# Tokens loaded first, squares summed on TensorE, modulation blocks moved between the first projection steps

## The chip, the cores and the metric

One core of a Trainium2 chip runs the whole program in one launch. The metric is the device time of that launch in microseconds (us). The kernel before takes 2099.12 us (median of 3 runs, 2098.18 to 2099.53). The profiled execution took 2101.66 us, and its span, from the first to the last instruction in the trace, is 2099.9 us.

The engines are named as in the profile: PE is TensorE's matrix multiplication and PEld its weight load, DVE is VectorE, ACT is ScalarE, POOL is GpSimd. SP only issues transfers, and POOL issues the stores.

## The reference

Two layers of a diffusion trunk over 128 context tokens and 1024 latent tokens of width 1024. Everything the change touches lies in the opening of layer 0:

```python
def rms_norm(x, g):
    y = xf * lax.rsqrt(jnp.mean(xf * xf, axis=-1, keepdims=True) + EPS)
    return (y * g.astype(jnp.float32)).astype(x.dtype)
def ada_mod(cvec, w, b):
    m = jax.nn.silu(cvec) @ w + b
    shift, scale, gate = jnp.split(m, 3, axis=-1)
...
hp = rms_norm(xp, norm_w[l]) * (1.0 + sc_p) + sh_p
hs = rms_norm(xs, norm_w[l]) * (1.0 + sc_s) + sh_s
...
z_a, xbc, dt_raw, u_b, g_b = jnp.split(h @ w_in, SPLIT_E, axis=-1)
```

and in the filter of the Hyena channels, which needs no token at all:

```python
hdn = jnp.sin(freq * (feats @ w1 + b1))
hdn = jnp.sin(freq * (hdn @ w2 + b2))
filt = (hdn @ w3).astype(f32)
```

## The kernel before

Tokens lie along the free axis: a tile is 128 channels by T = 1158 columns (the context, two zero columns, the latents, four zero columns), and there are eight such tiles `x[0]` to `x[7]`, called `hl` in the trace because they sit in the buffers that later hold the low halves. Each float32 operand of a large product is split into a high and a low part, so a product is three matmuls (L158 to L160 in `proj`, L185 to L187 in `proj_step`).

The opening (L1444 to L1506) does these things, in this order of issue:

- `silu_wide` prepares the conditioning vectors (`cw`).
- `filter_mlp` is a generator with the two small layers of the filter's network. `KM = (-1, 2)` runs the first layer before everything else and the second one in the middle of the loop over the tokens. A layer is six matmuls (L401, L412), then `sin_layer` on DVE (L377 to L383) and the sine on ACT (L384). The second layer ends with its result split into `hdh` and `hdl` (L418, L419), from which all the filter's later work starts.
- Eight blocks of the modulation's weights, 1 MB each in two halves, are loaded by `load`. Block order is `(0, 4, 1, 5, 2, 6, 3, 7)`: a shift block and the scale block of the same two channel tiles. `ada` multiplies a block with `cw` (L288, 16 matmul records) and copies the row out (L294); `cols` turns rows into columns with a selection matrix (L304) and adds the bias on DVE (L307, and L311 for a scale).
- Blocks 0 to 3 are loaded alternately with the tokens: two halves of a block, then two token tiles, and so on.
- For each token tile ACT squares it (L1485) and DVE adds the square to `xacc` (L1487), seven additions one after the other.
- `rstd_rep` sums `xacc` over the partitions with nine matmuls that have one column each (L324, 18 records), turns the sums into 1/sqrt on POOL (`pow`, L330), and spreads the result over all partitions with three diagonal products (L336 on DVE, L339 on PE, copies L343 to L347 on ACT) into `rep`. Its argument `fill` slips `cols` and the fifth block between.
- For k = 0 to 7, `make_h` forms the normalized and modulated tile k: a product on DVE (L356), the high part on ACT (L361), the low part on DVE (L362), two zero stretches on POOL (L365, L366). `proj_step` then multiplies it with slices of the first two weight chunks, 18 matmuls per step. `cols` runs in each step, and `ada` in the first three.

Then comes the stage `xbc`: the first two chunks are evacuated and convolved (L582 to L594, L695, L696), and ten more chunks of 72 matmuls follow. Beside it a list of generators (`self.bg`) is advanced, one step for each third of a chunk (`tick`, rate `RX` = 1.0): `filter_groups`, eight groups of the filter (L496 to L571), ending each with a store to `Hd` on POOL's queue. When `xbc` is through, `drain` empties the list, the buffers of the filter are given back, and the stage `z` begins, whose own background work loads the remaining modulation weights (`wa`) into memory that the filter held.

PSUM has two pools: three banks `pj`, and five banks `bg` that the second chunk of the first projection shares with everything else. Each engine runs its own instructions strictly in the order in which they stand. That order is set by the tile framework's scheduler from the order of the code and its own estimates.

Of the kernel before, what the change touches and what calls it, by code (L numbers as in the profile page):

```python
# [9 lines left out]
AF = mybir.ActivationFunctionType  # L10
# [5 lines left out]
D = 1024  # L16
# [20 lines left out]
def tk(c):  # L37
    return 0 if c == 0 else OFF + 128 * (c - 1)
# [6 lines left out]
class Net:  # L45
    XE = "vector"
    MID, RA = 2, 2.5
    KM, RX = (-1, 2), 1.0
    NT, EX, RO, RH, RS, RZ = 1, 3, 1.6, 1.7, 1.4, 2.0
# [263 lines left out]

    def rstd_rep(self, acc, pool, ncnt, tag="tt", fill=()):

# [4 lines left out]
        nc = self.nc  # L320
        p = self.ps()
        one = self.ones[0:acc.shape[0], 0:1]
        for c in range(NCH):
            nc.tensor.matmul(p[:, c:c + 1], acc[:, tk(c):tk(c) + 128], one, start=True, stop=True)  # L324
        for f in fill[:-3]:
# [8 lines left out]
        for g in range(3):  # L334
# [10 lines left out]
            else:  # L345
                o = tk(3 * g)
                nc.scalar.copy(rep[:, o:o + 384], q[:, :384])  # L347
        return rep

    def make_h(self, l, k, x, rep, slot):  # L350
# [20 lines left out]
    def sin_layer(self, arg, src, bcol, fcol, pool):  # L371
# [11 lines left out]
        nc.vector.tensor_scalar(out=arg, in0=arg, scalar1=3.1415925, scalar2=-3.1415925, op0=ALU.min, op1=ALU.max)  # L383
        nc.scalar.activation(arg, arg, AF.Sin)  # L384

    def filter_mlp(self, keep, pool):
# [31 lines left out]
        nc.scalar.copy(hi, b)  # L418
        nc.vector.tensor_tensor(out=lo, in0=b, in1=hi.bitcast(F32), op=ALU.subtract)  # L419
        self.hdn = hi, lo  # L420

    def stage_a(self, s, d, rd, qd, A, pool, tag):
# [1000 lines left out]
    def run(self, upto="end"):  # L1423
# [19 lines left out]
        self.nraw = 0  # L1443
        mlp = self.filter_mlp(p_hf, p_fg)  # L1444
        self.bg.append(self.filter_groups(p_fg))
        with self.pool("x0") as px:
            x = [self.t(self.p_h, [128, T], f"hl{k}") for k in range(8)]
            self.silu_wide(px)
            acc = self.t(px, [128, T], "xacc")
            blocks = (0, 4, 1, 5, 2, 6, 3, 7)  # L1450
            raws = []

            def load(n):
                if n < 4:
                    r = [self.t(self.p_h, [128, 1024], f"hh{(2 * n + h) % 6}") for h in range(2)]
                elif n == 6:
                    r = [self.t(p_fg, [128, 1024], "u8", bufs=self.nu8) for h in range(2)]
                else:
                    t = self.t(p_fg, [128, 2048], "A") if n == 7 else self.t(p_fg, [128, 2304], "F", bufs=2)
# [3 lines left out]
                raws.append(r)  # L1463

            rows = []

            def ada(n):
                rows.append(self.ada_block(blocks[n], raws[n], px))

            def cols():  # L1470
                while rows:
                    self.ada_cols(*rows.pop(0))

            if -1 in self.KM:
                next(mlp)
            for n in range(4):
                load(n)
                for k in (2 * n, 2 * n + 1):
                    self.dma(x[k], self.i["xT"][:, k])
            for n in range(4):  # L1480
                cols()
                ada(n)
                for k in (2 * n, 2 * n + 1):
                    sq = self.t(self.p_h, [128, T], f"hh{6 + k % 2}") if k else acc
                    nc.scalar.activation(sq, x[k], AF.Square)  # L1485
                    if k:
                        getattr(nc, self.XE).tensor_tensor(out=acc, in0=acc, in1=sq, op=ALU.add)  # L1487
                if n in self.KM:
                    next(mlp, None)
            self.w_load(0)  # L1490
            load(4)
            load(5)
            self.w_load(1)
            load(6)
            load(7)
            self.load_tf(p_hf)
            nop = lambda: None
            rep = self.rstd_rep(acc, px, D, "xacc", [cols, lambda: ada(4), nop, nop, nop])
            self.ps0 = [[self.pj() for b in range(3)], [self.ps() for b in range(3)]]
            first = [(None, self.w_next(), p) for p in self.ps0]  # L1500
            for k in range(8):
                self.make_h(0, k, x[k], rep, (px, [128, T], "sq") if k % 2 else (self.p_h, [128, T], "hh7"))
                cols()
# [341 lines left out]
```

## Time and profile before

| | |
|---|---|
| median of 3 runs | 2099.12 us |
| profiled execution | 2101.66 us, span 2099.9 us |
| PE busy from 0 to 50 us | 27.2 of 50 us with gaps of up to 8.6 us |
| PE busy from 100 to 400 us | 297.4 of 300 us |
| DVE busy from 100 to 180 us | 74.6 of 80 us |
| matrix clock over the span | 0.989 of full |

How to read the profile: it is one execution recorded by the hardware. A row of the timeline gives the start in us, the duration in us, the engine, the line of the kernel, the operation, the tile written and the tiles read, how many instructions were merged into the row, and in brackets the idle time ahead of it and what ended it. A table by stretches gives the busy us of each engine with the number of instructions, then the granted clock of PE (PEclk, 1.00 is full) and what the transfers did. On PE one matmul of float32 shows as two records; a busy PE may still be slow, because its clock may be halved.

### The profile page before, as it was taken

To read this page: it belongs to the slowest core of one execution; us is meant where nothing else is said; L and a number is where in the kernel's file an instruction comes from. 1 tells how busy PE (TensorE), PEld (TensorE's weight loads), DVE (VectorE), ACT (ScalarE), POOL (GpSimd) and SP (SyncE) were. 2 spreads that over 40 slices of the span, in tenths; PEclk is the share of its full clock that TensorE was granted. 3 is DMA by queue.
4 is the path that set the end of the run, shared out by engine and by line. 5 is a ranking of instruction groups with operands and counts; after the bars stand their busy time and mean duration, and the time that the engine had idled before them with its cause. 6 is when DMAs were issued, how large, how long until landed. Compare 5 with 4: busy or idle time off the path is not lost.

```text
span 2099.9 us, 33885 instructions
## 1 busy us (share of the span) xinstructions
PE 2041.4 (97%) x13088; PEld 1839.9 (88%) x13088; DVE 1316.7 (63%) x2774; ACT 908.3 (43%) x2031; POOL 120.4 (6%) x241
## 2 busy tenths in 40 slices
PE   5999999999999999999999999999999999999998
PEld 2899998889999999888887899898888888888977
DVE  5797745135778788898899774644444344454464
ACT  3576552252333332554466512434445454453231
POOL 1110001110000000000000000200000000000000
PEclk8999999999999999999999999999999999999999
DMA  8133339654121213343353451423333223333462
GB/s 331 52 124 102 117 142 294 222 178 158 67 92 57 79 57 101 139 129 124 116 178 102 136 167 41 121 71 91 91 116 88 77 79 96 110 115 111 124 225 81
DMA packets 115417, 257.36 MB, mean 123 GB/s; under 512 B 27159, under 2 KB 63639, under 8 KB 112791
## 3 DMA queue, kind: packets, MB, share of 16 engines
q1 hardware_dynamic: 99880, 192.01, 28.8%
q0 software_dynamic: 15376, 63.18, 8.4%
q8 instruction: 104, 1.70, 0.3%
q14 instruction: 57, 0.47, 0.1%
HBM read 187.25 MB, written 67.89 MB: 121 GB/s over the span
## 4 chain that ended last, share of the span: by engine, by line
PE 36%; issue 20%; DVE 3%; DMA 2%; ACT 1%; POOL 1%; SPq 0%; POOLq 0%; DVEq 0%; ACTq 0%
PE pj L158 7%; PE pj L159 7%; PE pj L160 7%; PE pj L1363 1%; PE pj L1364 1%; PE pj L1362 1%; PE bg L989 1%; PE bg L1023 1%; PE bg L1002 1%; PE bg L1325 1%; PE bg L1337 1%; PE bg L914 1%; PE pj L186 1%; PE bg L1308 1%; PE pj L187 0%
## 5 line engine op out<-in xcount | busy, mean ns | idle before, releaser
L158 PE MATMUL pj<-hh,whi 128*128 128x386 f32 x1728 | 604.2, 350 | 0.8 <-DVE acc L846 0.8
L159 PE MATMUL pj<-hl,whi 128*128 128x386 f32 x1728 | 590.0, 341 | 0.0
L160 PE MATMUL pj<-hh,wlo 128*128 128x386 f32 x1728 | 589.5, 342 | 0.0
L158 PEld LDWEIGHTS pj<-hh,whi 128*128 128x128 f32 x1728 | 326.2, 189 | 21.4 <-issue 18.0
L159 PEld LDWEIGHTS pj<-hl,whi 128*128 128x128 f32 x1728 | 326.5, 189 | 7.4 <-issue 6.3
L160 PEld LDWEIGHTS pj<-hh,wlo 128*128 128x128 f32 x1728 | 326.1, 189 | 5.3 <-issue 4.5
L131 DVE TENSOR_TENSOR wlo<-wraw,whi 128x1024 fp32r<-128x1024 f32 x108 | 131.9, 1222 | 162.3 <-ACT whi L130 162.0
L130 ACT CAST whi<-wraw 128x1024 fp32r<-128x1024 f32 x108 | 113.2, 1049 | 257.5 <-PE pj L159 222.7
L1241 DVE CUSTOM_DVE_ANT_0 sz<-bg,Tb 128x512 f32<-128x512 f32 x128 | 83.5, 688 | 128.0 <-PE bg L1308 127.5
L582 ACT COPY raw<-pj 128x386 f32<-128x386 f32 x105 | 50.6, 483 | 166.0 <-PE pj L160 76.6
L1243 ACT ACTIVATE sz<-sz,mx 128x512 f32<-128x512 f32 x128 | 91.5, 716 | 56.9 <-DVE mx L1241 56.6
L159 PE MATMUL pj<-ylo,whi 128*128 128x386 f32 x324 | 111.7, 345 | 0.0
L158 PE MATMUL pj<-yhi,whi 128*128 128x386 f32 x324 | 110.1, 340 | 0.0
L160 PE MATMUL pj<-yhi,wlo 128*128 128x386 f32 x324 | 109.7, 339 | 0.0
L1339 ACT COPY Pt<-bg 128x512 f32<-128x512 f32 (+1 forms) x144 | 71.9, 549 | 32.0 <-PE bg L1337 28.2
L1163 PE MATMUL pj<-whi,hh 128*128 128x256 f32 x288 | 83.4, 291 | 0.0
L1164 PE MATMUL pj<-wlo,hh 128*128 128x256 f32 x288 | 81.9, 285 | 0.0
L1165 PE MATMUL pj<-whi,hl 128*128 128x256 f32 x288 | 81.2, 282 | 0.0
L1337 PE MATMUL bg<-csq,sz 128*128 128x128 f32 x528 | 73.8, 280 | 0.0
L907 ACT ACTIVATE xw<-xt,wd 128x64 f32<-128x64 f32 x256 | 64.6, 336 | 8.3 <-PE bg L914 8.2
L1337 PEld LDWEIGHTS bg<-csq,sz 128*128 128x128 f32 x528 | 56.6, 140 | 13.0 <-issue 12.7
L1080 DVE SCALAR_TENSOR_TENSOR x<-pj,mod,x 128x128 f32<-128x128 f32 (+1 forms) x96 | 46.4, 513 | 28.1 <-PE pj L160 23.7
(424 smaller groups left out, 4061.3 us busy)
## 6 DMA issues: line engine op xcount, KB each, us to landing
wraw<-in_we SPq DMA_DIRECT2D x52, 512.0 KB, 3.6
wa<-in_wada SPq DMA_DIRECT2D x32, 512.0 KB, 6.9
wraw<-in_wo SPq DMA_DIRECT2D x24, 512.0 KB, 3.7
Tb<-Cd SPq DMA_DIRECT2D x256, 48.0 KB, 2.0
Hd<-H POOLq DMA_DIRECT2D x8, 1280.0 KB, 5.9
H<-Hd SPq DMA_DIRECT2D x8, 1280.0 KB, 6.6
xt<-xtd SPq DMA_DIRECT2D x17, 512.0 KB, 4.2
wraw<-in_woe SPq DMA_DIRECT2D x16, 512.0 KB, 3.5
```

Of the source, the lines that this page charges most:

```text
L130: self.nc.scalar.copy(hi, r)
L131: self.nc.vector.tensor_tensor(out=lo, in0=r, in1=hi.bitcast(F32), op=ALU.subtract)
L158: nc.tensor.matmul(p[:, :NB], wh, xh[k][:, sl], start=(k == 0), stop=False)
L159: nc.tensor.matmul(p[:, :NB], wh, xl[k][:, sl], start=False, stop=False)
L160: nc.tensor.matmul(p[:, :NB], wl, xh[k][:, sl], start=False, stop=(k == nk - 1))
L1163: nc.tensor.matmul(p[:, :256], self.hh[k][:, ts], hi[:, q:q + 256], start=(k == 0), stop=False)
L1164: nc.tensor.matmul(p[:, :256], self.hh[k][:, ts], lo[:, q:q + 256], start=False, stop=False)
L1165: nc.tensor.matmul(p[:, :256], self.hl[k][:, ts], hi[:, q:q + 256], start=False, stop=(k == 7))
L1241: V.tensor_tensor_reduce(out=z[:, :n], in0=s, in1=tb, scale=-1.0, scalar=3.0e38, op0=ALU.add, op1=ALU.min, accum_out=m1)
L1243: nc.scalar.activation(z[:, :n], z[:, :n], AF.Exp, bias=m1, scale=-1.0, accum_out=sm)
L1337: nc.tensor.transpose(pt[:, b * 128:(b + 1) * 128], p[:, b * 128:(b + 1) * 128], self.ident)
L1339: nc.scalar.copy(t[:, :nb * 128], pt[:, :nb * 128])
```

## The change

Seven edits, all in the opening of layer 0 and in the generator of the filter's network:

1. All eight token tiles are loaded ahead of the modulation's weights. Behind them come blocks 0 and 1, the first weight chunk, block 2, the second weight chunk, blocks 3, 4, 5 and 7; block 6 and the filter's tables are issued in step 2 of the projection. The blocks go to other buffers.
2. The squares are no longer added up in `xacc`. Squares 0 to 5 are added in pairs on DVE, and each pair, then square 6 and square 7 alone, goes to PE: `token_sums` is nine one-column matmuls that all accumulate in one PSUM bank. There are five such groups instead of one.
3. `ada(0)`, `ada(1)` and their `cols` come between the sums and the diagonal products; `ada(2)` to `ada(7)` come in pairs in steps 0, 2 and 4, `cols` in steps 1, 3, 5 and 7.
4. The filter's generator has more stops: the first sine is issued behind the squares, and the second layer runs in the background of `xbc`, ahead of `filter_groups`, with an empty step in its middle.
5. The rows of `ada` have a tag of their own (`row`, two buffers).
6. `rstd_rep` takes ready sums in its argument `p`.
7. The knobs `XE` and `KM` go.

```diff
-        row = self.t(pool, [128, 256], "w3")
+        row = self.t(pool, [128, 256], "row", bufs=2)
...
+    def token_sums(self, p, sq, first, last):
+        for c in range(NCH):
+            self.nc.tensor.matmul(p[:, c:c + 1], sq[:, tk(c):tk(c) + 128], self.ones[:, 0:1], start=first and c == 0, stop=last,
+                                  skip_group_check=True)
...
         self.sin_layer(a, src, hp[:, 0:1], hp[:, 2:3], pool)
         yield
+        nc.scalar.activation(a, a, AF.Sin)
+        yield
...
         self.sin_layer(b, src, hp[:, 1:2], hp[:, 2:3], pool)
+        yield
+        yield
+        nc.scalar.activation(b, b, AF.Sin)
...
+        self.bg.append(mlp)
         self.bg.append(self.filter_groups(p_fg))
...
+            next(mlp)
+            for k in range(8):
+                self.dma(x[k], self.i["xT"][:, k])
+            load(0)
+            load(1)
+            self.w_load(0)
+            load(2)
+            self.w_load(1)
+            for n in (3, 4, 5, 7):
                 load(n)
...
+            p = self.ps()
+            for k in range(8):
+                last, sq = (sq if k else None), self.t(self.p_h, [128, T], f"hh{(6, 7, 0, 1)[k % 4]}")
+                nc.scalar.activation(sq, x[k], AF.Square)
+                if k in (1, 3, 5):
+                    nc.vector.tensor_tensor(out=sq, in0=sq, in1=last, op=ALU.add)
+                if k % 2 or k == 6:
+                    self.token_sums(p, sq, k == 1, k == 7)
+            next(mlp)
...
-            rep = self.rstd_rep(acc, px, D, "xacc", [cols, lambda: ada(4), nop, nop, nop])
+            rep = self.rstd_rep(None, px, D, "xacc", [lambda: ada(0), lambda: ada(1), cols, nop, nop, nop], p)
...
-                cols()
-                if k < 3:
-                    ada(k + 5)
+                if k % 2:
+                    cols()
+                elif k < 6:
+                    ada(k + 2)
+                    ada(k + 3)
+                if k == 2:
+                    load(6)
+                    self.load_tf(p_hf)
```

The changed file's lines are some lines off: L351 is the sums, L287 and L303 stand for L288 and L304 (`ada`, `cols`), L337 for L339, L326 for L328, L306 and L310 for L307 and L311, L334 for L336, L381 to L387 for L377 to L383, L417 for L412, L157 to L159 for L158 to L160, L601 to L705 for the convolution, L526 to L528 for the filter's first product (L517 to L519).

**The front, PE.** From the last block ahead of the sums to the first diagonal product, in the kernel before (`xacc` is the added squares, `F` the fifth block, `bg` a PSUM bank):

```order
L288 MATMUL bg_272<-hh_51_180,cw_129 32x256 x4
L288 MATMUL bg_272<-hh_52_181,cw_129 32x256 x4
L324 MATMUL bg_310<-csq_72,xacc_132 128x1 x9
L304 MATMUL bg_320<-sel_7_82,w_75_281 128x2 x2
L288 MATMUL bg_325<-F_291,cw_129 32x256 x8
L339 MATMUL bg_345<-diag_343,csq_72 128x384
```

The same place in the changed kernel, behind the first layer of the filter's network (`hh_59` to `hh_65` are the squares, `hh_44` to `hh_47` the halves of blocks 0 and 1):

```order
L351 MATMUL bg_197<-csq_72,hh_59_200 128x1 x9
L351 MATMUL bg_197<-csq_72,hh_61_214 128x1 x9
L351 MATMUL bg_197<-csq_72,hh_63_228 128x1 x9
L351 MATMUL bg_197<-csq_72,hh_64_240 128x1 x9
L351 MATMUL bg_197<-csq_72,hh_65_251 128x1 x9
L287 MATMUL bg_263<-hh_44_168,cw_129 32x256 x4
L287 MATMUL bg_263<-hh_45_169,cw_129 32x256 x4
L287 MATMUL bg_274<-hh_46_172,cw_129 32x256 x4
L303 MATMUL bg_285<-sel_7_82,row_272 128x2 x2
L287 MATMUL bg_274<-hh_47_173,cw_129 32x256 x4
L303 MATMUL bg_289<-sel_7_82,row_283 128x2 x2
L337 MATMUL bg_303<-diag_301,csq_72 128x384
```

Five groups of sums stand where one stood, and two blocks with their two selections stand between the sums and the diagonal products, where one selection and one block stood.

**The front, DVE.** From the sums' result (`ms`) to the diagonals in the kernel before:

```order
L307 TENSOR_TENSOR mod_5_80<-bg_320,pv_74 128x4
L328 TENSOR_SCALAR ms_336<-bg_310 128x9
L311 SCALAR_TENSOR_TENSOR mod_5_80<-mod_5_80,pv_74 128x4
L332 MEMSET xacc_340 128x2
L333 MEMSET xacc_340 128x4
L131 TENSOR_TENSOR wlo_366<-wraw_289,whi_365 128x1024
L336 TENSOR_TENSOR diag_343<-csq_72,rs_338 128x384
```

and in the changed kernel:

```order
L326 TENSOR_SCALAR ms_294<-bg_197 128x9
L306 TENSOR_TENSOR mod_5_80<-bg_285,pv_74 128x4
L306 TENSOR_TENSOR mod_5_80<-bg_289,pv_74 128x4
L310 SCALAR_TENSOR_TENSOR mod_5_80<-mod_5_80,pv_74 128x4
L334 TENSOR_TENSOR diag_301<-csq_72,rs_296 128x384
```

The first diagonal now stands behind the columns of both blocks (`mod`).

**The start of `xbc`, PE and DVE.** Here the changed kernel has the second layer of the filter's network. On PE the last matmul of the layer (L417, read from `H_150`, the first layer's result) stands inside the third chunk:

```order
L158 MATMUL pj_1051<-hl_94_337,whi_688 128x386
L159 MATMUL pj_1051<-hh_93_336,wlo_689 128x386
L417 MATMUL bg_708<-H_150,w_37_136 64x384 x2
L157 MATMUL pj_1051<-hh_100_389,whi_688 128x386
L158 MATMUL pj_1051<-hl_101_390,whi_688 128x386
```

and 42 rows of projection further on comes the first matmul that reads the layer's result `hdh`:

```order
L158 MATMUL pj_1113<-hl_134_624,whi_882 128x386
L159 MATMUL pj_1113<-hh_133_623,wlo_883 128x386
L526 MATMUL bg_755<-w3h_744,hdh_722 128x256
L526 MATMUL bg_768<-w3h_744,hdh_722 128x256
L526 MATMUL bg_781<-w3h_744,hdh_722 128x256
```

On DVE the layer's `sin_layer` (`H_711`, `A_712`) stands there mixed with the second chunk's convolution (`acc_734`) and a weight split (`wlo`):

```order
L381 TENSOR_SCALAR H_711<-bg_708,hp_132 128x384
L601 SCALAR_TENSOR_TENSOR acc_734<-raw_733,cvah_686,acc_734 128x1157
L383 TENSOR_SCALAR A_712<-H_711 128x1152
L603 SCALAR_TENSOR_TENSOR acc_734<-raw_733,cvah_686,acc_734 128x1157
L384 TENSOR_SCALAR A_712<-A_712 128x1152
L130 TENSOR_TENSOR wlo_1141<-wraw_886,whi_1140 128x1024
L385 SCALAR_TENSOR_TENSOR H_711<-A_712,H_711 128x1152
L705 SCALAR_TENSOR_TENSOR acc_734<-raw_733,acc_734 128x1158
L386 SCALAR_TENSOR_TENSOR H_711<-A_712,H_711 128x1152
L387 TENSOR_SCALAR H_711<-H_711 128x1152
```

In the kernel before, the same layer stood in the opening, and its place on PE here held nothing but projection and filter matmuls, since `hdh` was long there:

```order
L384 ACTIVATE H_253<-H_253 128x1152
L418 CAST hdh_264<-H_253 128x1152
L294 COPY w_90_334<-bg_325 128x256
L343 COPY xacc_340<-bg_345 128x128
L344 COPY xacc_340<-bg_345 128x256
```

(these are rows of ACT, ahead of the first copy of `rep`).

**The passage from `xbc` to `z`, PE.** In the kernel before the first halves of the later modulation weights (`wa`) stand apart:

```order
L677 MATMUL bg_3104<-csq_72,acc_2983 128x128
L288 MATMUL bg_3166<-wa_3154,cw_3151 32x256 x4
L158 MATMUL pj_3171<-hh_143_646,whi_3011 128x386
L159 MATMUL pj_3171<-hl_144_647,whi_3011 128x386
L160 MATMUL pj_3171<-hh_143_646,wlo_3012 128x386
L288 MATMUL bg_3166<-wa_3156,cw_3151 32x256 x4
```

In the changed kernel the last filter group's matmuls stand 23 projection matmuls ahead of the end of `xbc` instead of 141, and halves 4 to 10 of `wa` stand in one piece, some 50 rows behind that end:

```order
L287 MATMUL bg_3240<-wa_3192,cw_3183 32x256 x4
L303 MATMUL bg_3276<-sel_7_82,row_3234 128x2 x2
L287 MATMUL bg_3286<-wa_3194,cw_3183 32x256 x4
L303 MATMUL bg_3321<-sel_7_82,row_3280 128x2 x2
L287 MATMUL bg_3286<-wa_3196,cw_3183 32x256 x4
L287 MATMUL bg_3331<-wa_3236,cw_3183 32x256 x4
L303 MATMUL bg_3358<-sel_7_82,row_3325 128x2 x2
L287 MATMUL bg_3331<-wa_3238,cw_3183 32x256 x4
L287 MATMUL bg_3368<-wa_3282,cw_3183 32x256 x4
L303 MATMUL bg_3395<-sel_7_82,row_3362 128x2 x2
L287 MATMUL bg_3368<-wa_3284,cw_3183 32x256 x4
L620 MATMUL pj_3299<-hh_93_336,wdts_3295 64x386
```

From the middle of the stage `z` on, PE has the same instructions in the same order in both kernels.

More of the change, by code (lines that the diff above doesn't have):

```diff
@@ L45 @@
 class Net:
-    XE = "vector"
     MID, RA = 2, 2.5
-    KM, RX = (-1, 2), 1.0
+    RX = 1.0
     NT, EX, RO, RH, RS, RZ = 1, 3, 1.6, 1.7, 1.4, 2.0
@@ L312, in ada_cols, with rstd_rep @@
                                            op0=ALU.add, op1=ALU.mult)
-    def rstd_rep(self, acc, pool, ncnt, tag="tt", fill=()):
+    def rstd_rep(self, acc, pool, ncnt, tag="tt", fill=(), p=None):
         fill = list(fill)
         nc = self.nc
[L321 to L324, printed above, removed]
+        if p is None:
+            p = self.ps()
+            self.token_sums(p, acc, True, True)
         for f in fill[:-3]:
@@ L383, in sin_layer @@
         nc.vector.tensor_scalar(out=arg, in0=arg, scalar1=3.1415925, scalar2=-3.1415925, op0=ALU.min, op1=ALU.max)
-        nc.scalar.activation(arg, arg, AF.Sin)
     def filter_mlp(self, keep, pool):
@@ L420, in filter_mlp @@
         self.hdn = hi, lo
+        yield
     def stage_a(self, s, d, rd, qd, A, pool, tag):
@@ L1448, in run @@
             self.silu_wide(px)
-            acc = self.t(px, [128, T], "xacc")
             blocks = (0, 4, 1, 5, 2, 6, 3, 7)
-            raws = []
+            raws = {}
             def load(n):
[L1454 to L1457, printed above, removed]
+                h = lambda k: self.t(self.p_h, [128, 1024], f"hh{k}")
+                u = lambda: self.t(p_fg, [128, 1024], "u8", bufs=self.nu8)
+                if n < 2:
+                    r = [h(2 * n + 2), h(2 * n + 3)]
+                elif n in (3, 6):
+                    r = [u(), u()]
+                elif n == 4:
+                    r = [u(), self.t(p_fg, [128, 1024], "sm")]
                 else:
-                    t = self.t(p_fg, [128, 2048], "A") if n == 7 else self.t(p_fg, [128, 2304], "F", bufs=2)
+                    t = self.t(p_fg, [128, 2048], "A") if n == 5 else self.t(p_fg, [128, 2304], "F", bufs=2)
                     r = [t[:, 0:1024], t[:, 1024:2048]]
@@ L1462, in load @@
                     self.dma(r[half], self.i["wada"][0, blocks[n], half])
-                raws.append(r)
+                raws[n] = r
             rows = []
             def ada(n):
-                rows.append(self.ada_block(blocks[n], raws[n], px))
+                rows.append(self.ada_block(blocks[n], raws.pop(n), px))
             def cols():
@@ L1472, in cols @@
                     self.ada_cols(*rows.pop(0))
-            if -1 in self.KM:
-                next(mlp)
-            for n in range(4):
-                load(n)
-                for k in (2 * n, 2 * n + 1):
-                    self.dma(x[k], self.i["xT"][:, k])
-            for n in range(4):
-                cols()
[L1482 to L1496, printed above, removed]
+            next(mlp)
[7 more added lines that the diff above has]
+            for n in (3, 4, 5, 7):
+                load(n)
+            p = self.ps()
+            for k in range(8):
[6 more added lines that the diff above has]
+            next(mlp)
             nop = lambda: None
-            rep = self.rstd_rep(acc, px, D, "xacc", [cols, lambda: ada(4), nop, nop, nop])
+            rep = self.rstd_rep(None, px, D, "xacc", [lambda: ada(0), lambda: ada(1), cols, nop, nop, nop], p)
             self.ps0 = [[self.pj() for b in range(3)], [self.ps() for b in range(3)]]
@@ L1502, in run @@
                 self.make_h(0, k, x[k], rep, (px, [128, T], "sq") if k % 2 else (self.p_h, [128, T], "hh7"))
-                cols()
-                if k < 3:
-                    ada(k + 5)
+                if k % 2:
[6 more added lines that the diff above has]
+                    self.load_tf(p_hf)
                 self.proj_step(first, self.hh, self.hl, k, 0, 7)
```

## The prediction

> **What bounds the kernel now.** I read the page first, then the busy time by stretches, then the timeline of the opening.
>
> ```profile
> span 2099.9 us, 33885 instructions
> PE 2041.4 (97%) x13088; PEld 1839.9 (88%) x13088; DVE 1316.7 (63%) x2774; ACT 908.3 (43%) x2031; POOL 120.4 (6%) x241
> ```
>
> PE is idle for 58.5 us in all. So an edit can pay in two ways only: fill PE's gaps, or take work off it. The stretches (busy us of PE, PEld, DVE, ACT, POOL, each with its instructions, then PEclk, transfers' share, GB/s) show where the gaps are:
>
> ```profile
> 0.00:10.00 10.00, 1.21 (x4) 0.53 (x6) 0.89 (x6) 1.50 (x2) 0.60 (x6) 1.00 0.59 174
> 10.00:20.00 10.00, 8.65 (x50) 3.71 (x46) 6.42 (x9) 4.16 (x5) 0.00 (x0) 1.00 1.03 415
> 30.00:40.00 10.00, 1.43 (x19) 0.81 (x17) 9.93 (x12) 3.43 (x4) 0.00 (x0) 0.62 1.02 407
> 40.00:50.00 10.00, 7.89 (x40) 5.97 (x40) 3.94 (x11) 2.70 (x4) 5.22 (x6) 0.50 0.82 326
> 100.00:120.00 20.00, 18.34 (x144) 17.94 (x143) 19.77 (x41) 14.00 (x40) 2.71 (x7) 1.00 0.20 57
> ```
>
> From 30 to 40 us DVE is full and PE empty; from 100 us on PE is full, DVE nearly so. The opening's chain, with the first and last projection records:
>
> ```profile
> 38.02 1.36 DVE L1487 TENSOR_TENSOR xacc<-xacc,hh 128x1158 f32<-128x1158 f32 x1
> 39.53 3.97 PE L324 MATMUL bg<-csq,xacc 128*128 128x1 f32 x18 [8.57 <-DVE xacc L1487]
> 43.36 0.99 PE L304 MATMUL bg<-sel,w 128*128 128x2 f32 x4
> 44.28 1.94 PE L288 MATMUL bg<-F,cw 128*32 128x256 f32 x16
> 44.78 2.81 POOL L330 TENSOR_TENSOR rs<-ms,mh 128x9 f32<-128x9 f32 x1 [43.61 <-DVE xacc L333]
> 47.62 1.03 DVE L336 TENSOR_TENSOR diag<-csq,rs 128x384 f32<-128x384 f32 x2 [1.72 <-POOL rs L330]
> 48.33 4.18 PE L339 MATMUL bg<-diag,csq 128*128 128x384 f32 x6 [2.11 <-DVE diag L336]
> 52.54 0.48 ACT L347 COPY xacc<-bg 128x384 f32<-128x384 f32 x1 [0.21 <-PE bg L339]
> 53.03 1.07 PE L288 MATMUL bg<-F,cw 128*32 128x256 f32 x16
> 53.22 1.28 DVE L356 SCALAR_TENSOR_TENSOR hh<-hl,mod,xacc 128x1024 f32<-128x1024 f32 x1
> 54.53 1.15 ACT L361 ACTIVATE hh<-hh,mod 128x1024 fp32r<-128x1024 f32 x1
> 55.82 0.88 PE L185 MATMUL pj<-hh,whi 128*128 128x386 f32 x3 [1.72 <-ACT hh L361]
> 62.94 0.45 PE L187 MATMUL bg<-hh,wlo 128*128 128x386 f32 x1
> 88.82 0.34 PE L187 MATMUL bg<-hh,wlo 128*128 128x386 f32 x1
> ```
>
> The last addition ends at 39.4, the sums at 43.5, the first projection matmul starts at 55.8 (12.3 later), the eight steps end at 89.0 (33.2 later). The change attacks the 39.4. The same modulation block takes 1.94 at 44.28 and 1.07 at 53.03: PE's clock is halved in between.
>
> ```profile
> 42.00:44.00 2.00, 2.00 (x11) 2.00 (x11) 0.00 (x0) 0.43 (x1) 0.00 (x0) 0.50 1.08 451
> 44.00:46.00 2.00, 2.00 (x18) 0.87 (x18) 1.51 (x6) 0.00 (x0) 1.22 (x1) 0.50 0.93 384
> 52.00:54.00 2.00, 2.00 (x21) 1.13 (x19) 0.86 (x2) 1.76 (x4) 0.00 (x0) 0.77 0.00 0
> ```
>
> From 42 to 46 PE's records leave no gap, yet the clock stays at 0.50; it comes back only at 52.9, behind 4.2 us of diagonal products. One-column sums, selections and modulation blocks did not raise it.
>
> **Part 1, the front.** By 10 us 1.74 MB have come (174 GB/s), about 0.85 of them constants. Eight token tiles are 4.74 MB, and at 415 GB/s the last is there at 10 + (4.74 - 0.89) / 0.415 = 19.3, with its signal about 20, tile 1 at 11.6. A square takes:
>
> ```profile
> 15.10 1.17 ACT L1485 ACTIVATE xacc<-hl 128x1158 f32<-128x1158 f32 x1
> 13.66 0.76 DVE L379 TENSOR_SCALAR A<-H 128x1152 f32<-128x1152 f32 x1
> ```
>
> The first pair is added on DVE behind this L379, at 14.4 to 15.8. From there PE has five groups of sums. One group is 3.97 at half clock, and I keep half clock, by the stretches above: 15.8 + 5 x 3.97 = 35.7. The squares keep ahead: square 5 must wait for group one (same buffer, 19.8), the sine follows it, squares 6 and 7 end at 25.8. So the sums end at **35.7 instead of 43.5**; PE takes DVE's place as the bound.
>
> Behind them the changed order is longer. Two blocks (1.94 each) and two selections (0.99 each) with a row copy (0.4) end at about 42.2, where selection and block ended late without delaying anybody: POOL's `pow` (2.81) ended at 47.59 and the first diagonal followed. Now the first diagonal stands behind both blocks' columns on DVE, at 42.4, 6.7 after the sums instead of 4.1. `pow` is over by 39.2, hidden. Diagonal to `rep` is 5.4 (47.62 to 53.02) as before: 47.8. On ACT a row copy (0.4) and the split of the second weight chunk (1.05) stand ahead of the first large high part, as the split did; first projection matmul at about **51.3 (55.8)**, 15.6 after the sums.
>
> The steps carry more: blocks 4.5 instead of 2, selections 12 halves instead of 6, i.e. 2.5 x 1.07 + 3 x 0.5 = 4.2 us. Step 6 also waits: its columns come from PE after step 4, and DVE then needs two tiles' products and low parts (1.28 + 0.35 each) while PE has one step of 18 x 0.178 = 3.2 us: 1.5 us. So 33.2 + 4.2 + about 1 = 38.3, and the steps end at **89.6 instead of 89.0: +0.6**. Almost nothing of the 7.8 us reaches the end.
>
> **Part 2, the second layer.** Its rows in the opening, with the convolution's that it now stands between:
>
> ```profile
> 25.59 3.83 PE L412 MATMUL bg<-H,w 64*64 64x384 f32 x10
> 29.46 0.68 DVE L377 TENSOR_SCALAR H<-bg,hp 128x384 f32<-128x384 f32 x1 [1.00 <-PE bg L412]
> 34.20 1.36 DVE L381 SCALAR_TENSOR_TENSOR H<-A,H 128x1152 f32<-128x1152 f32 x1
> 40.09 1.16 ACT L384 ACTIVATE H<-H 128x1152 f32<-128x1152 f32 x1 [5.58 <-DVE H L383]
> 41.28 1.15 ACT L418 CAST hdh<-H 128x1152 fp32r<-128x1152 f32 x1
> 88.60 1.23 DVE L131 TENSOR_TENSOR wlo<-wraw,whi 128x1024 fp32r<-128x1024 f32 x1 [3.45 <-ACT whi L130]
> 90.52 1.42 DVE L592 SCALAR_TENSOR_TENSOR acc<-raw,cvah,acc 128x1157 f32<-128x1157 f32 x1
> 96.25 1.37 DVE L696 SCALAR_TENSOR_TENSOR acc<-raw,acc 128x1158 f32<-128x1158 f32 x1 [0.53 <-ACT raw L695]
> ```
>
> Ten records took 3.83 at half clock; at full clock the 12 are 2.3 us. Half of them fall into step 6's wait, half into a full PE: **+1.1** (bounds 0 and 2.3).
>
> The costly part is a wait. DVE's three L381 overwrite the buffer that the layer's last matmul reads; in the trace the first of them (29.46) starts only when the last L412 ends (29.42). From there, in the order shown, DVE has 3 x 0.68 + 2 x 1.42 + 1.37 + 1.23 and of the layer 0.76 + 0.75 + 2 x 1.36 + 0.75: 12.5, less 0.08 of overlap at each of 11 joints, 11.6. Then ACT: sine 1.16, a convolution copy 0.6, the cast to `hdh` 1.15, in all **14.5**. PE meanwhile has 42 projection records, 42 x 0.178 = 7.4, and then stands in front of its first matmul on `hdh`. Nothing passes it on PE: it waits 7.1, wherever the front ends. The 1.7 us that PE lost between 100 and 120 belonged to the first filter groups crowding DVE, and should go, for the groups start later: **+5.4** (bounds +3 and +8.5).
>
> **Part 3, the passage to `z`.** Four more background steps put the last filter group at the end of `xbc`.
>
> ```profile
> 299.12 0.39 PE L483 MATMUL bg<-A,tf 128*128 128x128 f32 x2
> 306.64 2.75 SPq L84 DMA_DIRECT2D wa<-in_wada  x6
> 326.53 0.64 PE L288 MATMUL bg<-wa,cw 128*32 128x256 f32 x8
> ```
>
> The weights `wa` are issued 7.1 after that group's last matmul, 20 us ahead of their use. Now that matmul stands 23 x 0.178 = 4.1 ahead of the end of `xbc`, so `wa` is issued 3.0 behind it. The first half lands about 3.6 later, the others every 1.26 (0.52 MB at 415 GB/s), the tenth 18 us behind the end. PE, never waiting, would want the first at 6.1 and the tenth at about 16.5; the projection behind it needs a transfer queued behind those ten. I take **+2.5** (0 if the queue is kinder, 6 at 310 GB/s).
>
> **Sum**, made against the profiled execution (2101.66, span 2099.9): 0.6 + 1.1 + 5.4 + 2.5 = **+9.6**, 2111.3. That execution is 2.5 above the median of the runs, so I predict 2099.1 + 9.6 = **2108.7**.
>
> **Rivals.** *Faster: the sums run at full clock and keep it.* A group would then be 2.2 (an L304 of 4 records takes 0.5 at full clock), the sums end 2.2 behind square 7, at about 27.5; chain and first step are shorter by 4.8 and 3.6, the steps end at about 72.7, -16.3. With the other terms -7.3: 2091.8. It decides when the clock rises before the third group. Against it: 42 to 46 above. For it: five groups in a row are longer than anything there.
>
> *The clock rises behind the first group and is lost again before the first step* (as it was between 52.9 and 56.3, when PE waited 1.7): sums end at 30.5, steps at 79.7, -9.3, in all about -0.4: 2098.7. The Trainium skill, in "TensorE: Matmul & The Clock Gate", section "What's actually happening", has PE go to full clock after about 3.4 us of sustained activity; by that rule it is this rival or the one above. Row 42 to 46 disagrees, unless one-column matmuls are no activity.
>
> *The wait for `hdh` is filled*, say by DVE running the layer earlier than I read: 2099.1 + 0.6 + 1.1 + 2.5 - 1.7 = 2101.6. Against it: the shared buffer and strict order.
>
> **How the numbers follow.** Forecast 0.60 (slower, its own range 2103.5 to 2115 from the bounds); full clock throughout 0.15, with a little for an unseen gain 0.18 faster; clock lost again 0.12 and wait filled 0.10, the same. About 0.2% (4.2 us) is what a measurement of this kernel can tell from no change. The range reaches from 2094 (between the two clock rivals) to 2115.
>
> **What would show it.** Right: five groups of L351 near 4 us each, clock 0.50, ending near 36; first projection near 51; its end near 90; a PE gap of about 7 near 108 to 115, released by ACT's cast of `hdh`; small PE waits for `wa` behind `xbc`. Wrong: groups of about 2 us, or no gap ahead of L526.

## The result, and the profile after

The changed kernel takes 2127.55 us (median of 4 runs, 2122.78 to 2130.90), the kernel before 2098.65 us (4 runs beside it). The ratio is 1.0138, with a 95% interval of 1.0116 to 1.0160. The change costs 28.9 us; the prediction said 9.6.

The head of the page of the changed kernel (span, then busy us of each engine):

```profile
span 2127.1 us, 34009 instructions
PE 2057.9 (97%) x13160; PEld 1856.3 (87%) x13160; DVE 1311.8 (62%) x2770; ACT 911.9 (43%) x2033; POOL 120.2 (6%) x241
```

The span is 27.2 us longer. PE is idle for 69.2 us instead of 58.5, and busy for 16.5 us more: four groups of sums are new (3.87 us each, in a stretch where it had been partly idle), and part of its later work ran at half clock.

To see where the time went, I lined up the two timelines by three marks that both kernels have: the last matmul of the eight projection steps (**a**), the first of the last nine transposes of `xbc` (**b**), and the eighteenth high-part cast of a weight block on ACT (**c**, inside `z`). From c on the distance stays within 3 us.

| | before | after | difference | predicted |
|---|---|---|---|---|
| a, steps end (start of last matmul) | 88.8 | 84.75 | -4.1 | +0.6 |
| b, last transposes of `xbc` | 325.4 | 338.0 | +12.6 | +3.2 |
| c, cast inside `z` | 406.7 | 433.7 | +27.0 | +9.6 |

Between b and c the changed kernel has 265 projection records (88, 88 and 89 of three kinds), the kernel before 243 (81 of each): 22 records of 0.178 us, 3.9 us, moved behind mark b. (The prediction put the end of `xbc` at +7.1; mark b stands 22 records earlier in the changed kernel, hence +3.2 in the table.) So `xbc` itself lost 12.6 + 3.9 + 4.1 = **20.6** and the passage to `z` 27.0 - 12.6 - 3.9 = **10.5**.

**The front**, timeline of the changed kernel (start, duration, engine, line, tiles, count, idle ahead and releaser):

```profile
16.09 19.36 PE L351 MATMUL bg<-csq,hh 128*128 128x1 f32 x90 [2.85 <-DVE hh L1503]
41.94 1.49 DVE L334 TENSOR_TENSOR diag<-csq,rs 128x384 f32<-128x384 f32 x3
42.64 3.78 PE L337 MATMUL bg<-diag,csq 128*128 128x384 f32 x6 [1.02 <-DVE diag L334]
46.35 1.07 PE L287 MATMUL bg<-F,cw 128*32 128x256 f32 x16
...
50.05 0.77 PE L184 MATMUL pj<-hh,whi 128*128 128x386 f32 x3 [2.20 <-ACT hh L365]
84.75 0.33 PE L186 MATMUL bg<-hh,wlo 128*128 128x386 f32 x1
```

Five groups in 19.36 us are 3.87 each, without a gap. That is half clock, although the table by stretches shows a full one there:

```profile
16.00:36.00 20.00, 19.91 (x98) 19.66 (x102) 6.81 (x8) 6.90 (x6) 1.00 (x7) 1.00 1.03 410
```

This trace has no clock record before 45.88 (the kernel before has none before 29.0), and without a record PEclk reads 1.00. The durations decide: the same group takes 2.17 at full clock (an experiment below shows it). The sums end at 35.45 (35.7 predicted). The first projection starts at 50.05 (51.3). Only the steps are clearly shorter than predicted: 35.0 us instead of 38.3.

**The start of `xbc`**, same view:

```profile
95.02 0.86 PE L417 MATMUL bg<-H,w 64*64 64x384 f32 x4
95.94 1.85 DVE L381 TENSOR_SCALAR H<-bg,hp 128x384 f32<-128x384 f32 x3 [2.57 <-PE bg L417]
104.11 1.36 DVE L705 SCALAR_TENSOR_TENSOR acc<-raw,acc 128x1158 f32<-128x1158 f32 x1
105.50 0.48 ACT L591 COPY raw<-pj 128x386 f32<-128x386 f32 x1 [3.12 <-DVE acc L705]
106.61 0.69 PE L157 MATMUL pj<-hh,whi 128*128 128x386 f32 x1 [6.82 <-ACT acc L592]
107.09 0.53 PE L158 MATMUL pj<-hl,whi 128*128 128x386 f32 x1
107.89 1.28 ACT L423 ACT_TABLE_LOAD   x1
110.81 1.15 ACT L426 CAST hdh<-H 128x1152 fp32r<-128x1152 f32 x1
112.28 0.75 PE L526 MATMUL bg<-w3h,hdh 128*128 128x256 f32 x5
132.90 1.09 PE L686 MATMUL bg<-csq,acc 128*128 128x128 f32 x4 [4.90 <-DVE F L532]
```

DVE's first third waits for the layer's last matmul, as predicted, and its chain with the convolution between follows. PE stands still for 6.82 us, but not in front of the filter's matmul: a projection matmul ahead of it needs a `pj` bank whose copy on ACT stands behind the convolution on DVE. Behind the wait each record takes 0.53 instead of 0.34. L526, the filter's matmul, then starts 0.3 behind the cast that it needs, with no wait of its own. A second wait of 4.90 follows at 128, in front of transposes that need a bank which DVE empties late.

**The clock.** Stretches of the changed kernel around these waits and the passage (busy us of PE, PEld, DVE, ACT, POOL with counts, then PEclk, transfers' share, GB/s):

```profile
98.00:112.00 14.00, 7.18 (x31) 6.86 (x30) 10.81 (x10) 8.65 (x11) 1.45 (x2) 0.76 0.26 80
127.00:142.00 15.00, 8.51 (x40) 6.15 (x38) 12.46 (x30) 10.36 (x28) 2.39 (x4) 0.66 0.20 57
340.00:366.00 26.00, 22.23 (x165) 15.01 (x164) 4.19 (x12) 4.97 (x12) 2.48 (x3) 0.93 0.97 368
366.00:382.00 16.00, 16.00 (x96) 13.37 (x95) 6.48 (x13) 2.26 (x5) 0.70 (x2) 0.89 0.53 128
390.00:406.00 16.00, 13.01 (x106) 9.26 (x106) 7.22 (x15) 6.45 (x23) 3.07 (x5) 1.00 1.04 349
```

Stretches of 1 us, summed from a to b, give 14.4 us of PE idle (2.55 before) and 5.55 us lost to half clock (none before): 11.9 + 5.55 of the 20.6. Of the 3.1 left, six of the layer's records take 1.6 from start to next start (two at 85.0, four at 95.0); the other 1.5 are not accounted for. From b to c they give 6.8 us of idle and 3.15 of half clock (none of either before). Not all of that half clock stands behind a wait: from 366 to 382 PE is busy for all 16.00 us, and the clock is at 0.50 from 373.6 to 377.0 (1.7 us lost), behind eighteen narrow records:

```profile
371.55 2.24 PE L628 MATMUL bg<-sel,dT 64*128 64x32 f32 x18
```

The kernel before has the same eighteen (2.19 us at 348.84) and keeps its clock. But four kernels of the experiments whose `wa` came early (`layer_in_opening`, `before_layer_in_steps` and the last two tried) lost the same 1.7 us at this place, with at most 0.3 us of idle between b and c. So this share needs no late transfer.

**The passage**, changed kernel (POOL's last store of the filter, SP's issue of `wa`, its first use), then sums of PE's waits from 290 to 430 (us, times, longest):

```profile
335.28 0.61 POOL L86 DMA_DIRECT2D Hd<-H  x1 [11.11 <-ACT H L570]
340.28 10.13 SPq L83 DMA_DIRECT2D wa<-in_wada  x9
344.57 0.64 PE L287 MATMUL bg<-wa,cw 128*32 128x256 f32 x8 [0.46 <-DMA wa<-in_wada]
...
PE bg L287 <- DMA wa<-in_wada: 4.1, 6, 1.1
PE bg L668 <- DVE adt L661: 1.5, 1, 1.5
```

The weights are issued at 340.3, 2.3 us behind mark b, where the kernel before issued them 18.8 us ahead of it.

### The profile page after: what moved, and what is told of

It reads as the page before. It is cut to its first block, busy times and chain, and to the rows that moved or that the text cites. A ratio compares the mean times of both kernels' runs of the same rounds, so it can differ in the third digit from the quotient of the medians.

```text
span 2127.1 us, 34009 instructions
## 1 busy us (share of the span) xinstructions
PE 2057.9 (97%) x13160; PEld 1856.3 (87%) x13160; DVE 1311.8 (62%) x2770; ACT 911.9 (43%) x2033; POOL 120.2 (6%) x241
## 5 line engine op out<-in xcount | busy, mean ns | idle before, releaser
L157 PE MATMUL pj<-hh,whi 128*128 128x386 f32 x1728 | 605.6, 350 | 7.8 <-ACT acc L592 6.8
L158 PE MATMUL pj<-hl,whi 128*128 128x386 f32 x1728 | 593.0, 343 | 0.0
L159 PE MATMUL pj<-hh,wlo 128*128 128x386 f32 x1728 | 591.6, 343 | 0.0
L157 PEld LDWEIGHTS pj<-hh,whi 128*128 128x128 f32 x1728 | 328.3, 190 | 29.6 <-issue 18.8
L158 PEld LDWEIGHTS pj<-hl,whi 128*128 128x128 f32 x1728 | 327.4, 189 | 8.2 <-issue 7.2
L159 PEld LDWEIGHTS pj<-hh,wlo 128*128 128x128 f32 x1728 | 328.0, 190 | 5.4 <-issue 4.5
L158 PE MATMUL pj<-ylo,whi 128*128 128x386 f32 x324 | 111.7, 345 | 0.0
L157 PE MATMUL pj<-yhi,whi 128*128 128x386 f32 x324 | 110.0, 340 | 1.5 <-DVE x L1089 1.5
L159 PE MATMUL pj<-yhi,wlo 128*128 128x386 f32 x324 | 109.7, 339 | 0.0
L1348 ACT COPY Pt<-bg 128x512 f32<-128x512 f32 (+1 forms) x144 | 71.9, 548 | 32.9 <-PE bg L1346 28.9
L1173 PE MATMUL pj<-wlo,hh 128*128 128x256 f32 x288 | 81.9, 285 | 0.0
L1089 DVE SCALAR_TENSOR_TENSOR x<-pj,mod,x 128x128 f32<-128x128 f32 (+1 forms) x96 | 46.4, 512 | 31.1 <-PE pj L159 26.7
```

What stands on the lines that cost most here:

```text
L157: nc.tensor.matmul(p[:, :NB], wh, xh[k][:, sl], start=(k == 0), stop=False)
L158: nc.tensor.matmul(p[:, :NB], wh, xl[k][:, sl], start=False, stop=False)
L159: nc.tensor.matmul(p[:, :NB], wl, xh[k][:, sl], start=False, stop=(k == nk - 1))
L1173: nc.tensor.matmul(p[:, :256], self.hh[k][:, ts], lo[:, q:q + 256], start=False, stop=False)
L1348: nc.scalar.copy(t[:, :nb * 128], pt[:, :nb * 128])
```

## The experiments

Ratios are against the kernel before, run on the same chip beside each (2097.6 to 2098.9 us); a, b, c are the marks above, as differences from the kernel before.

### Undo the move of the layer

```diff
-        self.bg.append(mlp)
...
-            for n in (3, 4, 5, 7):
-                load(n)
+            load(3)
+            load(4)
...
-            next(mlp)
+            for _ in mlp:
+                pass
+            load(5)
+            load(7)
```

> The changed kernel with the second layer of the filter's network run whole in the opening again (blocks 5 and 7 are loaded behind it, since it uses block 5's buffer); everything else as changed. My theory: all of the loss comes from moving that layer into xbc. Then the two gaps of PE in xbc (99.8 to 106.6 and 128.0 to 132.9, 11.9 us of idle time more than before and 5.6 us of halved clock) and the late weights behind xbc (13.3 us) go together; the layer's 10 records cost the opening up to 4 us, so the steps end at 86 to 89. About 2098, between 2095 and 2101. Rival: the loss comes from the other edits (block 6 and the tables issued late, the row buffers, the order of the blocks), and only the first gap goes: 2115 or more.

2105.91 us, ratio 1.0033 (1.0023 to 1.0043); a +5.2, b +5.7, c +7.7. The layer runs whole behind the squares here, and not as before in the middle of the loop over the tokens. `xbc` loses 0.6 instead of 20.6 and the passage 2.0 (1.7 of it the half clock above): both losses belong to the layer's place. The stretches of this run:

```profile
100.00:120.00 20.00, 19.86 (x145) 18.93 (x144) 19.53 (x42) 14.95 (x42) 2.06 (x4) 1.00 0.19 64
120.00:140.00 20.00, 19.03 (x122) 17.91 (x121) 18.44 (x36) 11.90 (x33) 2.76 (x7) 1.00 0.36 133
```

The size was missed at the other end: in this opening the layer costs 9.2 us against the changed kernel, not 4. Its matmuls stand between the sums at half clock, and its work on DVE and a weight split stand ahead of the first diagonal:

```profile
34.96 2.82 PE L417 MATMUL bg<-H,w 64*64 64x384 f32 x6
37.70 4.00 PE L351 MATMUL bg<-csq,hh 128*128 128x1 f32 x18
50.56 3.64 PE L337 MATMUL bg<-diag,csq 128*128 128x384 f32 x6 [2.69 <-DVE diag L334]
58.71 0.77 PE L184 MATMUL pj<-hh,whi 128*128 128x386 f32 x3 [2.64 <-POOL hl L370]
```

So edits 1 to 3, with the layer in the opening behind the squares, do not pay either: the steps end 5.2 later than before.

### The move of the layer alone

```diff
-    KM, RX = (-1, 2), 1.0
+    KM, RX = (-1,), 1.0
...
+        self.bg.append(mlp)
```

(with edit 4's extra stops of the generator.)

> The kernel before with the fourth edit alone: the second layer runs in the background of xbc ahead of the filter's groups. My theory: it gains what the layer's work in the opening cost there (0 to 6 us) and loses the two gaps and the passage to z, 31 us in all: 2122 to 2130. Rival: the loss needs the new front too; then the time stays under 2110.

2121.50 us, ratio 1.0108 (1.0091 to 1.0125); a -7.6, b +10.1, c +21.6. The same two waits are there:

```profile
50.10 1.03 PE L185 MATMUL pj<-hh,whi 128*128 128x386 f32 x3 [2.64 <-ACT hh L361]
102.77 0.69 PE L158 MATMUL pj<-hh,whi 128*128 128x386 f32 x1 [5.86 <-ACT acc L587]
129.74 1.08 PE L681 MATMUL bg<-csq,acc 128*128 128x128 f32 x4 [4.94 <-DVE F L527]
```

The front gains more than the changed kernel's (-4.1): without the layer, the old front is 3.5 us faster than the new one. Its first projection starts at 50.10, where the changed kernel's starts at 50.05. So edits 1 to 3 gained nothing up to there beyond what moving the layer alone gains, and the old front's steps are shorter (31.1 instead of 34.7 us to mark a).

### A faster background

```diff
-    RX = 1.0
+    RX = 1.15
```

> The changed kernel with the background's rate in xbc raised from 1.0 to 1.15, so that the filter's 36 steps are done some 30 us ahead of the end of xbc, as before. My theory: the passage to z loses 13.3 us only because the weights wa are issued behind the end of xbc; it goes, the two gaps in xbc stay (a little different in size): about 2114, 2110 to 2118. Rival: the passage is limited by the transfers whenever they are issued, and the time stays at 2124 or more.

2121.69 us, ratio 1.0112 (1.0097 to 1.0127); a -3.8, b and c both +17.2.

```profile
133.33 1.19 PE L560 MATMUL bg<-F,tcf 128*128 128x128 f32 x4 [4.89 <-issue]
323.83 3.46 SPq L83 DMA_DIRECT2D wa<-in_wada  x6
```

Both waits in `xbc` are there again (the first with 6.82). With the weights issued 18.8 us ahead of b again, the passage loses nothing. The lateness of that issue is the cause of nearly all of its loss: the kernels with early weights lose 0 to 2.0 there. `xbc` loses 21.0 (20.6). The total was missed by 7.7: 2.8 are the difference between the 13.3 that I had ascribed to the passage and its 10.5, some 3 came back behind c (the trace ends 20.2 later than that of the kernel before, c 17.2), and the rest is not accounted for.

### Late groups without the layer

```diff
+        self.bg.append(iter((0, 0, 0)))
         self.bg.append(self.filter_groups(p_fg))
```

(on top of the first experiment: three empty steps and the end of the iterator, the four steps that the layer takes.)

> The kernel with the layer in the opening (2105.9 us), with four empty steps put ahead of the filter's groups in the background of xbc: the groups come as late as in the changed kernel, but no layer runs there. Theory S (the lateness of the groups makes the second gap and the late weights): the second gap of PE (4.9 us, and some 3 us of halved clock behind it) and the passage (10.5 instead of 2.0) come back, the first gap does not: 2105.9 + 8 + 8.5 = about 2122. Theory D (the layer's own work on DVE, queued ahead of the first group, makes the second gap): only the passage comes back, 2113 to 2117.

2113.34 us, ratio 1.0074 (1.0057 to 1.0091); a +2.0, b -2.4, c +12.5. (Mark a differs by 3.2 from the first experiment's, although only the background of `xbc` was edited; why is not known.) With the 3.9 of moved records `xbc` loses nothing (-0.5) and the passage 11.0. Its stretches and waits (PE's waits over the first 460 us):

```profile
120.00:140.00 20.00, 20.00 (x165) 19.14 (x164) 18.61 (x39) 16.50 (x45) 4.05 (x5) 1.00 0.53 188
PE bg L287 <- DMA wa<-in_wada: 4.0, 3, 2.1
```

No second wait: theory S falls. Late groups alone make the passage's loss; the second wait needs the layer's work in `xbc`.

### The layer in a buffer of its own

```diff
-        b = self.t(pool, [128, 2560], "H")[:, 0:1152]
-        self.sin_layer(b, src, hp[:, 1:2], hp[:, 2:3], pool)
+        b = self.t(pool, [128, 2304], "F", bufs=2)[:, 0:1152]
+        self.sin_layer(b, second, hp[:, 1:2], hp[:, 2:3], pool)
```

(`second(g)` issues the two matmuls of a third; DVE takes that third over before the next is issued.)

> The changed kernel with the second layer still in the background of xbc, but its result in buffer F instead of H, which its own matmuls still read: each third is taken over by DVE as soon as its two matmuls are done, and its bank is free again. Theory B (the first gap comes from the shared buffer: DVE's first third waited for the last matmul, which waited for the second chunk's banks until 95.0): the layer is through before the steps end or shortly behind, the first gap (6.8 us and 2.3 us of halved clock) goes, perhaps the second too (4.9 and 3.2); the passage stays: 2110 to 2119. Theory C (DVE has too much to do there whatever the buffer): the time stays at 2124 or more.

2124.54 us, ratio 1.0122 (1.0109 to 1.0135); a -1.8, b +10.1, c +24.8: `xbc` loses 15.8 instead of 20.6.

```profile
81.89 0.68 DVE L381 TENSOR_SCALAR F<-bg,hp 128x384 f32<-128x384 f32 x1 [0.91 <-PE bg L416]
103.77 0.86 PE L525 MATMUL bg<-w3h,hdh 128*128 128x256 f32 x5 [2.08 <-ACT hdh L425]
111.83 0.45 PE L157 MATMUL pj<-hh,whi 128*128 128x386 f32 x1 [1.98 <-ACT acc L591]
```

The first third is taken over at 81.9 instead of 95.9, and the one long wait becomes several of about 2 us, now also ahead of the filter's matmul. The shared buffer, with the thirds handed over together, was about a quarter of the loss. The rest stays with the layer in `xbc`; that it comes from the layer's work among the convolutions on DVE and ACT is what is left by elimination. Theory C is nearer.

### The clock and the sums

Two kernels add wide matmuls whose result is not read. The first:

```diff
+            self.heat(4)
...
+                if k == 0:
+                    self.heat(2, sq)
...
                     self.token_sums(p, sq, k == 1, k == 7)
+                    self.heat(1, sq)
```

(and one behind each of the first two modulation blocks.)

> The changed kernel with idle wide matmuls (128x512, into a bank that is not read) added: four from about 3 us on, two behind the first square, one behind each group of sums and behind each of the first two modulation blocks. Theory A: PE's clock rises after wide matmuls and a group of sums then takes about 2.2 instead of 3.9; sums end near 29 instead of 35.5 and the steps 6 to 10 us earlier: 2117 to 2122. Theory B: windows with one-column sums lose the full clock again whatever stands beside them; groups stay near 3.9, each wide matmul costs 1.7 more at half clock: about 2136.

2131.57 us, ratio 1.0158 (1.0141 to 1.0174); a +4.3. The second has the same four at the start and five wide matmuls behind the first square, and none later:

> The changed kernel with idle wide matmuls only ahead of the sums: four from about 4 us on and five behind the first square, so that no gap of PE is left before the first group. The groups then begin at full clock. Theory P (one-column sums do not hold the clock): the first group or two take 2.2 to 3, the others 3.9 again; sums end at 33 to 36, time 2125 to 2130. Theory Q (only the 3.1 us gap ahead of the first group lost it): all five take about 2.2, paced by the squares; sums end near 29, time about 2120.

2125.40 us, ratio 1.0136 (1.0117 to 1.0154); a -4.9. Its first PE rows:

```profile
3.85 5.56 PE L352 MATMUL pj<-csq 128*128 128x512 f32 x8 [3.85 <-DMA csq<-in_c_sq]
9.35 2.15 PE L410 MATMUL bg<-F,w 33*64 33x384 f32 x12
11.43 4.56 PE L352 MATMUL pj<-hh,csq 128*128 128x512 f32 x10
16.54 2.17 PE L357 MATMUL bg<-csq,hh 128*128 128x1 f32 x18 [0.55 <-DVE hh L1515]
19.87 14.53 PE L357 MATMUL bg<-csq,hh 128*128 128x1 f32 x72 [1.17 <-DVE hh L1515]
```

Wide matmuls raise the clock (the filter's first layer takes 2.15 instead of 4.10), the first group of sums runs in 2.17, and the next four take 3.63 on the average: by the clock's records it is full from 7.64 to 21.30, falls 1.4 us into the stretch of four groups, and is at 0.50 until 45.2. A gap of 1.17 stands ahead of that stretch, so the fall alone does not show that sums lose the clock; but gaps of 1.3 and 1.4 among projection records lost none (`groups_one_step_later`), and 13 us of sums without a gap did not bring it back. In the first kernel one wide matmul (1.85 of every 5.5 us) between the groups did not bring it back either; the groups took 3.84. So theory P holds, and both clock rivals of the prediction fall. (Theory B of the first kernel had the groups right and its time 4 us too long.) The Trainium skill, in "TensorE: Matmul & The Clock Gate", section "What's actually happening", lets about 3.4 us of sustained activity release the throttle. The 19.36 us of one-column sums without a gap in the changed kernel disagree; the wide matmuls here, which start at 3.85 and have full clock from 7.64, agree.

### Attempts at a faster kernel

The layer in step 3 of the projection (in its own buffer), in the kernel before:

```diff
                     ada(k + 5)
+                if k == 3:
+                    next(mlp, None)
```

> The kernel before with the second layer moved to step 3 of the first projection, its result in buffer F so that each third frees its bank at once; nothing else changed. The opening should gain the 7.6 us that moving the layer out gained in the run with the fourth edit alone, the layer's 12 records cost 2.3 us of a full PE, and xbc and the passage lose nothing, since the groups start where they did: 2098 - 7.6 + 2.3 + about 1 = about 2094, 2091 to 2097. Rival: DVE, 73% busy in those steps, cannot take the layer's 8 us, PE waits for low parts, and the time is 2098 to 2102.

2101.53 us, ratio 1.0017 (1.0007 to 1.0026); a -3.6, b 0.0: the time of the rival. The same in the changed kernel, with all squares added on DVE, and `ada(0)`, `ada(1)` and `cols()` ahead of the sums:

```diff
-                if k in (1, 3, 5):
+                if k:
...
-                if k % 2 or k == 6:
-                    self.token_sums(p, sq, k == 1, k == 7)
+            ada(0)
+            ada(1)
+            cols()
+            self.token_sums(p, sq, True, True)
```

> The changed kernel with the second layer in step 3 of the projection (as in the run above), all eight squares added on DVE with one group of sums, and blocks 0 and 1 with their columns ahead of that group, so that the first diagonal product waits for the sums alone. The additions should end near 28.5, the sums near 32.5 instead of 35.5, the first diagonal start near 37 instead of 42.6, the first projection near 45 instead of 50; the steps then end near 82 (before 89.2): about 2091, 2088 to 2096. Rival: the squares come no sooner, because ACT or DVE holds them up, or the modulation blocks are not there in time; then the first projection stays near 50 and the time is about 2097.

2099.19 us, ratio 1.0011 (1.0000 to 1.0022); a -4.1, b 0.0, c +0.3. Its rows, then the stretch behind the steps:

```profile
30.13 3.98 PE L351 MATMUL bg<-csq,hh 128*128 128x1 f32 x18
39.08 4.18 PE L337 MATMUL bg<-diag,csq 128*128 128x384 f32 x6 [4.97 <-DVE diag L334]
46.81 0.77 PE L184 MATMUL pj<-hh,whi 128*128 128x386 f32 x3 [0.69 <-POOL hl L370]
...
104.00:108.00 4.00, 1.52 (x8) 1.52 (x8) 4.00 (x15) 2.67 (x6) 0.00 (x0) 0.84 0.00 0
```

The first projection starts 9.0 us earlier than before (1.8 later than expected), but the layer in the steps and the blocks moved there leave 4.1 at a, and these are lost when PE waits for DVE, which is full (4.00 of 4.00), and then for its clock. Three more kernels tried to get past that:

```diff
+        self.bg.append(iter(()))
         self.bg.append(self.filter_groups(p_fg))
```

> The kernel with tokens first, sums on DVE and the layer in the steps (2099.2 us), the filter's groups one background step later. There the 4 us gained by the end of the steps were lost again in a gap of PE at 104 to 109 behind the first group's work on DVE, with halved clock behind it. Theory: a step (7 us) later the group's work no longer stands ahead of the bank copies that PE waits for, the gap goes, the passage loses nothing yet (weights 12 us ahead of the end of xbc): 2093 to 2096. Rival: the gap moves along with the group: 2099 to 2103.

2100.11 us, ratio 1.0005 (0.9997 to 1.0014); a -4.6, b -0.1. The one gap became three of 1.0 to 1.4 us and some shorter ones, 6.3 us of idle from a to b in all, with no clock lost. Then two steps in all, with `RX = 1.06`:

> The same with two background steps more ahead of the groups and the rate raised from 1.0 to 1.06, so that the last group ends about where it did. By the theory of the run above 2093 to 2096; by the rival 2099 or more; if the higher rate crowds DVE as the rate of 1.15 did (3.4 us), in between.

2100.66 us, ratio 1.0006 (0.9995 to 1.0016); b -0.6. And three wide matmuls behind the sums on top of it:

> The run above with three idle wide matmuls behind the sums, where PE has nothing to do for 5 us. They cost nothing there and should raise the clock ahead of the diagonal products, which then take 2.2 instead of 4.2, and the modulation block behind them 1.1 instead of 1.9: the first projection starts 1 to 2.5 us sooner, the time is 0 to 2.5 us less than the run above. If the clock is given by fixed windows of 3.4 us that must be filled (as the transitions at multiples of 3.4 us suggest), the gain is 0 or about 2, depending on where the window falls.

2099.79 us, ratio 1.0010 (1.0001 to 1.0018); a -6.1, b -2.0, c -0.2.

```profile
34.78 4.51 PE L336 MATMUL pj<-csq,dz 128*128 128x512 f32 x6 [0.69 <-ACT dz L333]
39.12 2.10 PE L346 MATMUL bg<-diag,csq 128*128 128x384 f32 x6
```

The diagonal products took 2.10 instead of 4.18, and the first projection came at 44.74 instead of the 46.52 of the run before it, 1.8 us sooner, as expected; the time did not change by more than these measurements can tell. None of the five beats the kernel before: what the front gains up to a, `xbc` gives back by c.

## Why the prediction was wrong, step by step

**Its sign was right, its size was a third of the cost.** One row of the kernel before, in its steps, is needed for the second point:

```profile
56.33:63.16 6.83, 6.83 (x23) 5.80 (x21) 5.40 (x9) 1.44 (x2) 1.76 (x4) 0.50 0.41 114
```

- *Sums at half clock, end at 35.7, first projection at 51.3*: right (35.45 and 50.05). The predicted PEclk of 0.50 could not be read there. The two clock rivals are refuted by the warmed kernels.
- *Steps end at 89.6*: 4.9 us too late. I carried over the 33.2 us of the kernel before. But 3.4 of these (33.4 us from the first matmul, 29.9 of work) were half clock between 56.3 and 63.2, which the trace of the kernel before showed (the row above) and which the new front avoids. 29.9, about 3.6 for the added 40 records of blocks and 12 of selections (4.2 predicted) and 1.6 for six of the layer's records make 35.1, against 35.0 measured; the wait of 1.5 at step 6 did not occur.
- *The second layer's matmuls, +1.1*: the twelve records took 3.2, all of it on a full PE: 1.6 in the steps, 1.6 in `xbc`.
- *The wait behind the layer, +5.4*: the step that failed first, and by the most: with the layer's records `xbc` was to lose at most 6.5, and it lost 20.6. The wait came at 99.8 instead of 108, ahead of L157 instead of L526; by the prediction's own sign (no gap ahead of L526) it was wrong. I had said that nothing passes the wait on PE, and overlooked that the projection itself needs banks that wait for the convolution on DVE. That its length, 6.82, is close to 7.1 is partly luck: it ended with the convolution and a copy on ACT, 4.2 us before the cast of `hdh` began. From DVE's first third to the end of that cast it took 16.0 instead of 14.5, with a table load of 1.28 on ACT that the sum lacked, and PE came to L526 9.0 late (16.5 us for 42 records of 0.178): 6.8 of wait, the rest half clock. More costly were two omissions. I took back 1.7 us of the old wait, because the groups start later; in its place came a wait of 4.90, which the layer's work in `xbc` causes (it is gone in both kernels with the layer in the opening, with the groups early or late). And I charged a wait with its length alone; half clock behind the two waits cost another 5.55.
- *The passage, +2.5*: the step that failed by the largest factor, and by 8.0 us. The mechanism was right: the late last group delays `wa`, which was issued 2.3 us behind mark b (predicted 3.0 behind the end of `xbc`), and an earlier issue takes the loss away. The size was 10.5. I had set PE's need against the arrival of ten halves. The waits for `wa` add up to 4.1; 2.7 of idle lie elsewhere (1.5 for `adt`); 3.15 are half clock, 1.7 of them with no wait ahead; 0.6 is not accounted for.
- *The rival "wait filled"* did not happen: PE lost the time ahead of L157. The range was 2103.5 to 2115; the bounds of the terms add up to a little more, 2102.7 to 2116.5. Both were too narrow, because both omissions had the same sign.

What stays open: which of the layer's instructions on DVE or ACT makes the second wait (its order was not tried), and why front gains up to a return to nearly the same b in several kernels. In the one shown, DVE is full where they are lost; that DVE is the limit in all of them was not tested.

## What to carry to other kernels

Price a wait on PE with its length plus what the clock loses behind it: two waits of 6.8 and 4.9 cost 5.55 more here. Half clock can also come without a wait, as behind the narrow matmuls here (1.7). Before moving work into a stage where PE is full, add up what DVE and ACT carry there, and look for every bank that stands behind them, not only for the moved work's own reader. And count what hangs on the last background step: four steps more than the stage could spare moved one transfer by 21 us and cost 10.5 in the next stage.

## What the runs showed of the hardware

- One-column matmuls do not bring PE's full clock: 19.36 us of them without a gap stayed at 3.87 a group. Begun at full clock, a group took 2.17 us and the next four 3.63 on the average. Wide ones (128x512) bring it: they began at 3.85, and the eight records (four matmuls) took 5.56 us, where one matmul (two records) takes 1.85 at half clock, by the first kernel with wide matmuls, and 0.91 at full clock (4.56 for five).
- Half clock does not need a wait: it followed eighteen records of 64x32 (2.24 us at 371.55) in a stretch where PE was busy all the time. The same eighteen at 348.84 in the kernel before were not followed by it.
- The clock changed on steps of 3.41 us: behind the wait at 99.8 it was halved for 6.8 us, behind the wait at 128 for 10.2, two and three times 3.41. The Trainium skill, in "TensorE: Matmul & The Clock Gate", section "What's actually happening", gives a free-running window of 3413 ns. The trace agrees.
